# A chunked recurrence on TensorE: where the small matmuls stand between the dense ones

## The chip, the core and the metric

The kernel runs on one core of one Trainium2 chip. The metric is device microseconds of one execution, from the first to the last instruction and what lies around them; lower is better. The median of three runs of the kernel before is 1153.91 us (1153.35 to 1154.5).

## The reference, cut to what matters

Two layers over 256 tokens of width 2048. The first mixes tokens by a recurrence over 32 heads of size 64, the second is a sparse attention that the change does not touch. Of the first, what counts here:

```python
r, k, v, z = (mixed[i] @ w_rkvz[i] for i in range(4))        # four dense 2048 x 2048 products
# per head, one step per token t:
sa = S @ a_t
S = S * w_t + outer(sa, b_t) + outer(v_t, k_t)
o_t = S @ r_t
# afterwards, per head and token:
o = normalise(o) * ln_g + ln_b
bonus = sum(r * k * r_k) * v                                 # a scalar per head and token, times v
y = (o + bonus) * silu(z)
h = x + y @ w_o
```

## The kernel before, in words

**Dense products.** Every large weight is fetched as f32 by SyncE (line 178), split by ScalarE into a high part `whi` (line 206) and by VectorE into the rest `wlo` (line 191). TensorE then makes three products for each pair of operands: lines 587 to 589 (256 columns, weight as the stationary operand) or 569, 570 and 572 (512 columns). All of these use the whole 128 x 128 array.

**The recurrence.** The 256 tokens are cut into four chunks `c` of 64, the 32 heads into eight units `U` of four. Inside a chunk the recurrence is written as matrix products on blocks of 64, with the inverse of a triangular 64 x 64 matrix, which VectorE computes beforehand (`stage_t`, lines 799 to 808; its second half still runs during units 0 to 2). The four heads of a unit are packed into the quarters of the array, so that these matmuls use tiles of 64 x 64 or 128 x 64 of the array. Each is f32 and stands as two records in the trace.

A unit is a loop over twelve steps `v`; `phase(U, c, p)` is called with `c = v // 3` and `p = v % 3`:

- p = 0: for c = 0 `removal` (line 1024, 128 x 64) and then the bonus, 16 matmuls with two columns each (line 1036, 64 x 64; its operand `mb` = r times k times r_k is made by VectorE on line 963). For c > 0 eight matmuls with the state S (line 1040, 64 x 64). Then ScalarE copies the result to X (line 1042).
- p = 1: four matmuls with the inverse Yb (line 1047, 64 x 64); ScalarE copies the result to `uv` (line 1049).
- p = 2: the output's part (line 1053), the next chunk's `removal` (line 1024) and the update of the state (line 1058), all 128 x 64. VectorE makes the next S (lines 1061, 1063), ScalarE its decayed copy (line 1068). VectorE then takes statistics of the chunk's output (`stats`, line 1077).

All the results of a unit lie in one pair of PSUM banks, `PBK[U]`, one bank for each `x`: columns 0 to 63 of a bank hold what X reads, 64 to 127 what `uv` reads, 128 to 191 the state's update, from 192 on four blocks of the output O, and 448 to 455 the bonus. Two such pairs take turns. The dense product r uses two other banks, `rps[0]` and `rps[1]`, which also serve the preparation of the next unit.

Beside the unit's own steps stand three kinds of work, put at steps by tables:

- `AUX`, the preparation of unit U + 1 (`prep`): `B0` and `B1` transpose the keys (three 128 x 128 transposes each, line 993, into `rps[0]`; ScalarE copies them on line 994), `G` and `Y` finish the inverse (lines 974 and 983, 64 x 64; ScalarE copies G's result to `gs`, line 976, before Y may start), `A0` and `A1` make the products of the chunk (lines 1007 and 1009, 64 x 64, 24 matmuls each), `M0` to `M2` mask them on VectorE (line 1015). `T` turns the finished output of unit U - 1 (`turn_y`, line 1118, 64 x 64).
- `NORM`, the normalisation of unit U - 1 on VectorE and ScalarE (`finish`, lines 1085 to 1111). Its last step `z` (line 1107) is what `T` waits for.
- `fill(n)`: n times three dense matmuls of 256 columns, or their worth of 512 columns. `FILL[v]` gives n for units 0 to 5, `FILLL` for unit 6, `FILLO` for unit 7. In units 0 to 6 the dense work is the product r of later units, in unit 7 the output product.

`scale_r` (lines 962 and 963, VectorE) reads `rps[0]` in step 1 and `rps[1]` in step 6, for the next unit.

During the recurrence each engine works in the order in which the code is written (`tc.manual_schedule`), SyncE's queue included. What an instruction waits for follows from the tiles that it reads and writes. Work in the background (the second half of the inverse) is put in by a planner, `Sched`: every piece of work adds its estimated cost to a clock `sch.t`, and `sch.pump()` issues the next step of the inverse when that clock has come to its due time.

Of the kernel before, what the change touches and what calls it, by code (L numbers as in the profile page):

```python
# [13 lines left out]
OP = mybir.AluOpType  # L14
# [3 lines left out]
T, D, NK = 256, 2048, 16  # L18
LORA = 96
CH = 64  # L20
NCH = T // CH
# [47 lines left out]
W1D, CXG = 5, 1  # L69
KPO = 3  # L70
KLAG = 2
AUX = {2: ("B0",), 3: ("G",), 4: ("B1", "Y"), 7: ("A0",), 9: ("A1",), 10: ("T", "M2"), 11: ("M0", "M1")}
NORM = {1: ("nmr", "v", "02"), 2: ("b",), 5: ("24",), 6: ("46",), 7: ("68",), 8: ("g", "+"), 9: ("z",)}
FILLL = (3, 4, 4, 0, 0, 5, 0, 0, 0, 0, 0, 0)
PROLOGUE = ("R0", "R1", 6, "G", "B0", 4, "I", "Y", "B1", 2, "V6", "A0", 2, "V9", "A1", "M2", "V9", "M0", "M1", 2)
ZHOOK = 9
PACES, PACE = (0.6, 1.8, 3.0, 3.0), [0.0]
FILL = (3, 4, 4, 0, 0, 5, 4, 0, 4, 0, 4, 4)
FILLO, LASTFILL = 4, 36
QZ = (0, 25, 24, 1, 2, 23, 22, 21, 3, 20, 19, 18, 4, 17, 16, 15, 14, 13, 12, 11, 10)  # L80
SQG, XPG, W2G = 0, 1, 0
ZB = 8
# [135 lines left out]
def hybrid_kernel(ctx: ExitStack, tc: tile.TileContext, a: dict, out: bass.AP):  # L218
    nc = tc.nc
    V, S, G, PE = nc.vector, nc.scalar, nc.gpsimd, nc.tensor  # L220
    sch = Sched()
# [164 lines left out]
    W0, A0, KA, RK, KVG, BG = [prm1[:, 16 * i:16 * i + 16] for i in range(6)]  # L386
# [450 lines left out]
    R = [slice(0, 64), slice(64, 128)]  # L837
    H = lambda x, h: R[h ^ x]
    NU = NK // 2
# [16 lines left out]
    def load_y(U, eng=G, qs=(1, 0)):  # L856
        sch.require(lambda: U // 4 in tdone)
        for q in qs:
            for x in range(2):
                for h in range(2):  # L860
                    at = 64 * (h ^ x) + 32 * q
                    eng.dma_start(Yb[U % 2][at:at + 32, x, :, 32 * q:32 * q + 32],
                                inverse(yvd[U // 4], ((2 * U + x) % 8) * 2 + h, q))
# [42 lines left out]
    one = lambda name, shape: scan.tile(shape, F32, name=name)  # L906
# [4 lines left out]
    AMR = [one(f"amr{i}", [128, 2, 2, NCH, 64]) for i in range(2)]  # L911
    ARS = [[one(f"ars{i}{x}", [128, 2, NCH - 1, 64]) for x in range(2)] for i in range(2)]
    BKT = [[one(f"bkt{i}{x}", [128, NCH - 1, 2, 64]) for x in range(2)] for i in range(2)]
    mb = one("mb", [128, 2, T])
    ones2 = one("ones2", [128, 2])
    PCH, PBK, OU, GY, GS, AT, XS, STA, SST, NRM = [{} for _ in range(10)]
    mm = dict(stop=True, skip_group_check=True)
    each = [(x, h) for x in range(2) for h in range(2)]
# [8 lines left out]
    def clear_uv(U):  # L927
        for h in range(2):
            G.memset(UV[U % 2][R[h], :, :, h, :], 0.0)
# [20 lines left out]
    def parts(U, x):  # L950
        t = SPL[U % 2][x]
        return (t[:, 0:512].rearrange("p (c x t) -> p c x t", c=NCH, x=2),
                t[:, 512:512 + NCH * (CH + 1)].rearrange("p (c t) -> p c t", c=NCH),
                t[:, SPW - 512:SPW - 256],
                t[:, SPW - 256:].rearrange("p (x c t) -> p x c t", x=2, c=NCH))

    def scale_r(U, x):
        if x == 0:
            PCH[U] = scan.tile([128, 2, NCH], F32, name="pc", bufs=3)
        BK, pp, kr, ar = parts(U, x)  # L960
        pr = rps[x][:, 0:256]
        V.tensor_tensor(ar[:, 1], c3(pr), pp[:, :, 1:], op=OP.mult)
        V.tensor_tensor(mb[:, x], pr, kr, op=OP.mult)
        G.tensor_copy(PCH[U][:, x], pp[:, :, CH])
        G.tensor_tensor(ARS[U % 2][x], ar[:, :, 1:, :],
                        pp[:, None, 0:NCH - 1, CH:CH + 1].to_broadcast([128, 2, NCH - 1, CH]), op=OP.mult)
# [51 lines left out]
    def view(U, c0, n):  # L1018
        return PBK[U].rearrange("p (x c) -> p x c", x=2)[:, :, c0:c0 + n]

    def removal(U, c):
        uv, px = UV[U % 2], view(U, 0, 64)
        for x, h in each:
            PE.matmul(px[H(x, h), x], AMA[U % 2][:, x, c, :], uv[:, x, c, h, :], start=True, **mm)

    def phase(U, c, p):
        uv, px, pu, pS = UV[U % 2], view(U, 0, 64), view(U, 64, 64), view(U, 128, 64)
        O = view(U, 192 + 64 * c, 64)
        st = SST[U][0] if c else None
        if p == 0:  # L1030
            if c == 0:
                removal(U, 0)
                for i in range(NCH):
                    for x, h in each:
                        o = x * 512 + 448 + 2 * i
                        PE.matmul(PBK[U][H(x, h), o:o + 2], mb[R[h], x, 64 * i:64 * i + 64], ones2[R[h]], start=False, **mm)
            else:
                for k, o in enumerate((px, O)):
                    for x, h in each:
                        PE.matmul(o[H(x, h), x], ARS[U % 2][x][R[h], k, c - 1, :], st[R[h], x, :], start=False, **mm)  # L1040
            X = scan.tile([128, 2, 64], F32, name="X", bufs=2)
            S.activation(X, px, AF.Copy)
            XS[U] = X
            sch.t += 350
        elif p == 1:
            for x, h in each:
                PE.matmul(pu[R[h], x], Yb[U % 2][H(x, h), x, c, :], XS[U][H(x, h), x, :], start=False, **mm)
            for h in range(2):
                S.activation(uv[R[h], :, c, h, :], pu[R[h]], AF.Copy)
            sch.t += 200  # L1050
        else:
            for x, h in each:
                PE.matmul(O[H(x, h), x], AMR[U % 2][:, h, x, c, :], uv[:, x, c, h, :], start=False, **mm)  # L1053
            if c < NCH - 1:
                removal(U, c + 1)
            if c < NCH - 1:
                for x, h in each:
                    PE.matmul(pS[R[h], x], BKT[U % 2][x][:, c, h, :], uv[:, x, c, h, :], start=False, **mm)
                nxt = scan.tile([128, 2, 64], F32, name="S", bufs=3)
                if c == 0:  # L1060
                    V.tensor_copy(nxt, pS)
                else:
                    V.tensor_tensor(nxt, SST[U][1], pS, op=OP.add)
                dec = None
                if c < NCH - 2:
                    dec = scan.tile([128, 2, 64], F32, name="sP", bufs=2)
                    for x in range(2):
                        S.activation(dec[:, x], nxt[:, x], AF.Copy, scale=PCH[U][:, x, c:c + 1])
                SST[U] = (nxt, dec)
            sch.t += 700  # L1070

    def stats(U, c):
        if c == 0:
            STA[U] = (scan.tile([128, 2, 4, 6], F32, name="sta", bufs=2), scan.tile([128, 2, 4, 2], F32, name="mv", bufs=2))
        sta = STA[U][0]
        for x in range(2):
            V.bn_stats(sta[:, x, c, :], view(U, 192 + 64 * c, 64)[:, x])
# [72 lines left out]
    def fill(n):  # L1150
        budget[0] += 3 * N256 * n
        while budget[0] > 1.0:
            c = next(dense)
            budget[0] -= c
            sch.t += c
            sch.pump()
# [38 lines left out]
    for U in range(NU):  # L1195
        PBK[U] = pair_tile(U % 2)
        P = U - 1
        PACE[0] = PACES[min(U + 1, 3)]
        for v in range(12):
            phase(U, v // 3, v % 3)  # L1200
            if v % 3 == 2:
                stats(U, v // 3)
            sch.pump()
            if v == 11:
                if U + 2 < NU:
                    load_y(U + 2, qs=(1,))
                finish(U, "rg")
            if v == 0:
                if U and U + 1 < NU:
                    load_y(U + 1, qs=(0,))  # L1210
                if U + 1 < NU:
                    clear_uv(U + 1)
                    load_v(U + 1)
                if U + 2 < NU:
                    load_spl(U + 2)
            if v == 1 and U + 1 < NU:
                scale_r(U + 1, 0)
            if v == 6 and U + 1 < NU:
                scale_r(U + 1, 1)
            if U:  # L1220
                for step in NORM.get(v, ()):
                    finish(P, step)
            for step in AUX.get(v, ()):
                if step == "T":
                    if U:
                        turn_y(P)
                elif U + 1 < NU:
                    prep(step, U + 1)
            if v == 9 and U % 4 == 0:
                load_gb(U)  # L1230
            if v == 8 and U + 2 < NU:
                load_a(U + 2)
            if v == 8:
                load_rows(vt, vd, U)
            if v == 9:
                load_rows(zt, zd, U)
            fill(FILLO if U + 1 == NU else FILLL[v] if U + 2 == NU else FILL[v])
            sch.pump()
    U = NU - 1
    fill(6)  # L1240
# [216 lines left out]
    pr = accp("PT")  # L1457
# [283 lines left out]
```

## Time and profile before

| | us |
|---|---|
| median of three runs | 1153.91 |
| the profiled execution | 1155.41 |
| its span, first to last instruction | 1153.6 |
| TensorE busy | 1119.0 (97%) |
| VectorE busy | 844.8 (73%) |
| ScalarE busy | 715.8 (62%) |
| GpSimd busy | 328.3 (28%) |
| granted TensorE clock, mean | 0.992 |

The units of the recurrence begin, by line 1024 of step 0, at 371.7, 397.1, 421.7, 448.2, 473.9, 497.5, 521.5 and 542.3 us of the span; the last ends at about 570 us. In the timeline a row is: start in us, duration in us, engine, line, operation, output <- inputs, the tile of the array that is used (for matmuls), the shape, and the number of records that were merged; in brackets the idle time of the engine before it and what ended that. The matmuls of one engine are pipelined, so starts say more than durations: from one start to the next is what a matmul costs.

### The profile page before, as it was taken

Reading aid. Unit: us, or ns where it says so; the run is one execution under the profiler, and the core shown is the slowest. Engines: PE = TensorE matmul, PEld = TensorE weight load, DVE = VectorE, ACT = ScalarE, POOL = GpSimd, SP = SyncE. Lnnn points to the kernel's source line nnn. Section 1 sums busy time; section 2 is a strip of 40 time slices with the busy share of each in tenths; the row PEclk is TensorE's granted clock in tenths of the full one; section 3 lists DMA queues with packets and bytes.
Section 4 is the critical chain, followed back from the end, with each engine's and each line's share of the span. In section 5 each row is a group of like instructions: output and inputs, shape, how many; then the busy total and the mean of one; then the engine's idle time right before and its main releaser. Section 6 shows DMA issues by size and latency. Waiting matters only on the chain.

```text
span 1153.6 us, 25609 instructions
## 1 busy us (share of the span) xinstructions
PE 1119.0 (97%) x9414; PEld 979.6 (85%) x9414; DVE 844.8 (73%) x1876; ACT 715.8 (62%) x1680; POOL 328.3 (28%) x420
## 2 busy tenths in 40 slices
PE   7999999999999999998999999999999999999996
PEld 7878899888988888887788888887989989988886
DVE  6999876689897886566567876764567888775564
ACT  5767777577764466554547766665566666665553
POOL 1300045424347555653000010100333333333011
PEclk8999999999999999998999999999999999999999
DMA  6558878777879878774467667675746354645752
GB/s 232 160 186 247 236 206 262 233 216 219 259 219 277 202 218 235 217 192 121 138 213 255 199 194 260 199 243 163 198 121 163 100 135 107 165 107 176 285 186 104
DMA packets 232413, 226.31 MB, mean 196 GB/s; under 512 B 50608, under 2 KB 180000, under 8 KB 231904
## 3 DMA queue, kind: packets, MB, share of 16 engines
q1 hardware_dynamic: 227392, 219.73, 64.3%
q0 software_dynamic: 4896, 4.95, 1.9%
q8 instruction: 74, 1.21, 0.4%
q14 instruction: 51, 0.42, 0.1%
HBM read 200.48 MB, written 24.15 MB: 195 GB/s over the span
## 4 chain that ended last, share of the span: by engine, by line
PE 79%; DVE 11%; issue 3%; ACT 3%; DMA 3%; POOL 0%; SPq 0%; ACTq 0%; POOLq 0%; DVEq 0%
PE bank L570 13%; PE bank L569 13%; PE bank L572 13%; PE bank L587 7%; PE bank L589 7%; PE bank L588 7%; PE bank L234 5%; DVE wlo L191 3%; PE pair L572 1%; PE pair L569 1%; PE pair L570 1%; DVE invX L805 1%; ACT whi L206 1%; PE pair L1053 1%; DVE mtmp L426 1%
## 5 line engine op out<-in xcount | busy, mean ns | idle before, releaser
L191 DVE TENSOR_TENSOR wlo<-wraw,whi 128x512 fp32r<-128x512 f32 (+2 forms) x616 | 438.6, 725 | 149.9 <-ACT whi L206 145.2
L206 ACT ACTIVATE whi<-wraw 128x512 fp32r<-128x512 f32 (+2 forms) x664 | 402.0, 619 | 205.6 <-PE bank L572 94.5
L587 PE MATMUL bank<-mh,whi 128*128 128x256 f32 (+1 forms) x800 | 235.4, 294 | 0.8 <-ACT whi L206 0.4
L570 PE MATMUL bank<-wlo,mh 128*128 128x512 f32 (+3 forms) x608 | 229.1, 379 | 2.1 <-DVE wlo L191 2.1
L588 PE MATMUL bank<-ml,whi 128*128 128x256 f32 (+1 forms) x800 | 227.7, 285 | 0.0
L572 PE MATMUL bank<-whi,ml 128*128 128x512 f32 (+3 forms) x608 | 227.6, 377 | 0.0
L589 PE MATMUL bank<-mh,wlo 128*128 128x256 f32 (+1 forms) x800 | 227.3, 285 | 0.0
L569 PE MATMUL bank<-whi,mh 128*128 128x512 f32 (+3 forms) x608 | 202.2, 378 | 0.8 <-ACT mh L419 0.8
L587 PEld LDWEIGHTS bank<-mh,whi 128*128 128x128 f32 (+1 forms) x800 | 151.3, 189 | 7.0 <-issue 0.9
L588 PEld LDWEIGHTS bank<-ml,whi 128*128 128x128 f32 (+1 forms) x800 | 151.7, 190 | 1.8
L589 PEld LDWEIGHTS bank<-mh,wlo 128*128 128x128 f32 (+1 forms) x800 | 151.4, 189 | 1.3
L570 PEld LDWEIGHTS bank<-wlo,mh 128*128 128x128 f32 x608 | 114.3, 188 | 20.6 <-DVE wlo L191 3.3
L572 PEld LDWEIGHTS bank<-whi,ml 128*128 128x128 f32 x608 | 114.4, 188 | 17.8 <-issue 0.4
L569 PEld LDWEIGHTS bank<-whi,mh 128*128 128x128 f32 x608 | 113.4, 188 | 18.9 <-ACT mh L419 1.0
L191 POOL TENSOR_TENSOR wlo<-wraw,whi 128x512 fp32r<-128x512 f32 (+2 forms) x48 | 62.4, 1301 | 190.4 <-ACT whi L206 158.6
L570 PE MATMUL bank<-wlo,kvh 128*128 128x512 f32 x192 | 76.9, 401 | 0.0
L572 PE MATMUL bank<-whi,kvl 128*128 128x512 f32 x192 | 76.1, 396 | 0.0
L569 PE MATMUL bank<-whi,kvh 128*128 128x512 f32 x192 | 67.4, 396 | 0.0
L419 ACT ACTIVATE mh<-mtmp 128x256 fp32r<-128x256 f32 x96 | 39.0, 411 | 21.8 <-DVE mtmp L426 20.6
L426 DVE SCALAR_TENSOR_TENSOR mtmp<-xx,prm,xn 128x256 f32<-128x256 f32 x96 | 47.8, 504 | 1.2 <-POOL xx L458 1.0
L570 PEld LDWEIGHTS bank<-wlo,kvh 128*128 128x128 f32 x192 | 36.1, 188 | 8.7 <-issue 0.4
L420 DVE TENSOR_TENSOR ml<-mtmp,mh 128x256 fp32r<-128x256 f32 x96 | 41.5, 440 | 1.4 <-ACT mh L419 1.3
(332 smaller groups left out, 1871.2 us busy)
## 6 DMA issues: line engine op xcount, KB each, us to landing
wraw<-in_a_w_rkvz_dram SPq DMA_DIRECT2D x128, 512.0 KB, 5.5
wraw<-in_kv_w_dram SPq DMA_DIRECT2D x48, 512.0 KB, 4.4
wraw<-in_b_w_in_dram SPq DMA_DIRECT2D x40, 512.0 KB, 4.2
wraw<-in_a_w_o_dram SPq DMA_DIRECT2D x32, 512.0 KB, 4.6
wraw<-in_b_w_o_dram SPq DMA_DIRECT2D x32, 512.0 KB, 4.3
spd<-sp SPq DMA_DIRECT2D x16, 642.0 KB, 5.6
spl<-spd SPq DMA_DIRECT2D x16, 642.0 KB, 5.9
wraw<-in_b_w_in_dram SPq DMA_DIRECT2D x24, 384.0 KB, 3.3
```

The lines of the kernel that those rows point to most:

```text
L191: eng.tensor_tensor(lv, src, hv.bitcast(F32), op=OP.subtract)
L206: self.nc.scalar.activation(hv, src, AF.Copy)
L234: return fn(*args, **kw)
L419: S.activation(h, src, AF.Copy)
L420: V.tensor_tensor(l, src, h.bitcast(F32), op=OP.subtract)
L426: V.scalar_tensor_tensor(m, xx[:, k, :], mu[:, k:k + 1], xn[:, k, 1:], op0=OP.mult, op1=OP.add)
L569: PE.matmul(o, mh[:, ts], wh[:, 0, :], start=k == ends[0], stop=False)
L570: PE.matmul(o, mh[:, ts], wl[:, 0, :], start=False, stop=False)
L572: PE.matmul(o, ml[:, ts], wh[:, 0, :], start=False, stop=k == ends[1])
L587: PE.matmul(o, wh[:, s, :], mh, start=k == 0 and first, stop=False, **kw)
L588: PE.matmul(o, wh[:, s, :], ml, start=False, stop=False, **kw)
L589: PE.matmul(o, wl[:, s, :], mh, start=False, stop=k == NK - 1, **kw)
```

## The change

The bonus leaves step 0 and stands in step 6, behind `phase` and ahead of the planner's pump, as a function of its own that adds 430 ns to the planner's clock. Its operand `mb` gets a second buffer, since unit U + 1 now writes it while unit U has not read its own. `B1` goes from step 4 to step 5. The dense work that stood in steps 6 and 11 goes to steps 8 and 10, one fill goes from step 5 to step 0; a unit's sum is unchanged (32, 16 and 48 fills). With no dense work in step 11, the last output product of a unit (line 1053) is followed at once by the first `removal` of the next unit (line 1024).

```diff
-AUX = {2: ("B0",), 3: ("G",), 4: ("B1", "Y"), 7: ("A0",), 9: ("A1",), 10: ("T", "M2"), 11: ("M0", "M1")}
+AUX = {2: ("B0",), 3: ("G",), 4: ("Y",), 5: ("B1",), 7: ("A0",), 9: ("A1",), 10: ("T", "M2"), 11: ("M0", "M1")}
...
-FILLL = (3, 4, 4, 0, 0, 5, 0, 0, 0, 0, 0, 0)
+FILLL = (4, 4, 4, 0, 0, 4, 0, 0, 0, 0, 0, 0)
...
-FILL = (3, 4, 4, 0, 0, 5, 4, 0, 4, 0, 4, 4)
-FILLO, LASTFILL = 4, 36
+FILL = (4, 4, 4, 0, 0, 4, 0, 0, 8, 0, 8, 0)
+FILLO, LASTFILL = (4, 4, 4, 4, 4, 4, 0, 4, 8, 4, 4, 4), 36
...
-    mb = one("mb", [128, 2, T])
+    mb = [one(f"mb{i}", [128, 2, T]) for i in range(2)]
...
-        V.tensor_tensor(mb[:, x], pr, kr, op=OP.mult)
+        V.tensor_tensor(mb[U % 2][:, x], pr, kr, op=OP.mult)
...
+    def bonus(U):
+        for i in range(NCH):
+            for x, h in each:
+                o = x * 512 + 448 + 2 * i
+                PE.matmul(PBK[U][H(x, h), o:o + 2], mb[U % 2][R[h], x, 64 * i:64 * i + 64], ones2[R[h]], start=False, **mm)
+        sch.t += 430
...
                 removal(U, 0)
-                for i in range(NCH):
-                    for x, h in each:
-                        o = x * 512 + 448 + 2 * i
-                        PE.matmul(PBK[U][H(x, h), o:o + 2], mb[R[h], x, 64 * i:64 * i + 64], ones2[R[h]], start=False, **mm)
...
+            if v == 6:
+                bonus(U)
             sch.pump()
...
-            fill(FILLO if U + 1 == NU else FILLL[v] if U + 2 == NU else FILL[v])
+            fill(FILLO[v] if U + 1 == NU else FILLL[v] if U + 2 == NU else FILL[v])
```

## The prediction

> **What bounds the kernel now.** I read the page first (busy time by engine, clock, queues), then the waits of PE over the recurrence, then the timeline of PE, ACT and DVE through whole units.
>
> ```profile
> span 1153.6 us, 25609 instructions
> PE 1119.0 (97%) x9414; PEld 979.6 (85%) x9414; DVE 844.8 (73%) x1876; ACT 715.8 (62%) x1680; POOL 328.3 (28%) x420
> ...
> q8 instruction: 74, 1.21, 0.4%
> ```
>
> PE is busy for 97% of the span, so a microsecond that leaves PE's own sequence shortens the kernel, unless another engine's result is then late. The waits of PE between 372 and 570 us, the eight units of the recurrence, come to only some 10 us (who waited for whom: total us, times, longest):
>
> ```profile
> PE pair L1040 <- issue: 2.0, 1, 2.0
> ...
> PE pair L1118 <- DVE O L1107: 1.7, 4, 0.8
> PE bank L1009 <- issue: 1.7, 2, 1.1
> PE bank L993 <- DVE mb L963: 1.6, 1, 1.6
> ```
>
> So the recurrence has little idle time to win; the change must shorten PE's own work. What it aims at is the price of changing the tile size. Here are three small groups between dense matmuls, in step 8 of unit 4 (start, duration, engine and line; x counts records, of which each small f32 matmul makes two):
>
> ```profile
> 489.06 0.45 PE L1053 MATMUL pair<-uv,amr 128*64 128x64 f32 x8
> 489.34 0.40 PE L1024 MATMUL pair<-uv,ama 128*64 128x64 f32 x8
> 489.57 0.40 PE L1058 MATMUL pair<-uv,bkt 128*64 128x64 f32 x8
> 489.91 0.38 PE L587 MATMUL bank<-mh,whi 128*128 128x256 f32 x1
> 490.13 0.28 PE L588 MATMUL bank<-ml,whi 128*128 128x256 f32 x1
> 490.25 0.28 PE L589 MATMUL bank<-mh,wlo 128*128 128x256 f32 x1
> ```
>
> Read the starts. The same four matmuls take 0.23 us when the next group has their size (489.34 to 489.57) and 0.34 when dense work follows: 0.11 for the change. The first dense matmul after it takes 0.22 against 0.12 for the next: 0.10 more. So a detour out of dense work costs 0.2 to 0.3 us beside its matmuls, and the change removes such detours.
>
> **Part a, the seam between two units.** Steps 10 and 11 of unit 4 and 0 of unit 5:
>
> ```profile
> 493.85 0.39 PE L587 MATMUL bank<-mh,whi 128*128 128x256 f32 x1
> ...
> 495.48 0.45 PE L1053 MATMUL pair<-uv,amr 128*64 128x64 f32 x8
> ...
> 497.49 0.45 PE L1024 MATMUL pair<-uv,ama 128*64 128x64 f32 x8
> 497.87 0.64 PE L1036 MATMUL pair<-ones,mb 64*64 64x2 f32 x32
> 498.44 0.39 PE L587 MATMUL bank<-mh,whi 128*128 128x256 f32 x1
> ...
> 499.71 0.34 PE L1047 MATMUL pair<-X,Yb 64*64 64x64 f32 x8
> ```
>
> From 493.85 to 499.71 are 5.86 us with 12, 12 and 9 dense matmuls. After the change: 24 dense, 1.63 (493.85 to 495.48) and 12 x 0.12 more, 3.07; L1053 and L1024 side by side, 0.28 and 0.34 by the rows of step 8; 12 dense, 1.63. Sum 5.32, 0.54 less, and it holds three dense matmuls more (0.36) that step 5 gives up. Gain 0.90 at each of the six seams from units 0|1 to 5|6: -5.4. At the seam 6|7 there is no dense work beside it and PE waits for DVE's masks anyway (row 544.44 below): 0. The bonus itself isn't gone but paid in part b.
>
> **Part b, the bonus in step 6.** Unit 4, and unit 6, which has no dense work between L1040 and L1047 and so shows the bare chain:
>
> ```profile
> 485.83 0.46 PE L1040 MATMUL pair<-S,ars 64*64 64x64 f32 x16
> ...
> 487.85 0.34 PE L1047 MATMUL pair<-X,Yb 64*64 64x64 f32 x8
> ```
>
> ```profile
> 533.42 0.46 PE L1040 MATMUL pair<-S,ars 64*64 64x64 f32 x16
> ...
> 533.99 0.28 ACT L1042 ACTIVATE X<-pair 128x128 f32<-128x128 f32 x1 [0.24 <-ACT whi L206]
> ...
> 534.32 0.34 PE L1047 MATMUL pair<-X,Yb 64*64 64x64 f32 x8 [0.45 <-ACT X L1042]
> ...
> 536.57 0.29 DVE L1063 TENSOR_TENSOR S<-sP,pair 128x128 f32<-128x128 f32 x1 [2.29 <-PE pair L1058]
> 536.77 0.35 DVE L1077 BATCH_NORM_STATS2 sta<-pair 128x6 f32<-128x64 f32 x2
> ...
> 537.18 0.46 PE L1040 MATMUL pair<-S,ars 64*64 64x64 f32 x16 [0.73 <-DVE sta L1077]
> ```
>
> Now L1040 to L1047 takes 2.02, of which 12 x 0.12 = 1.44 is dense work that moves to step 8, where it only lengthens a dense run: 0.58 remains. Afterwards the bonus, 32 records, stands there: 0.57 (497.87 to 498.44) less 0.11 for the change at its end, 0.46. What decides is whether it runs while ACT makes X, or after it. X ends 0.85 after L1040's start (533.42 to 533.99 + 0.28), and L1047 can start at 0.90. The bonus writes columns 448 to 455 of the same PSUM bank of which X reads columns 0 to 63. Two places show that this kernel orders such neighbours by bank, not by column: the last L1040 above starts at 537.18, 0.06 after the statistics of other columns ended (537.12), though its own operand S was ready at 536.86; and in step 0 X waits for the whole bonus:
>
> ```profile
> 498.67 0.28 ACT L1042 ACTIVATE X<-pair 128x128 f32<-128x128 f32 x1 [0.97 <-PE pair L1036]
> ```
>
> L1024, whose columns X reads, had ended at 497.94, the bonus at 498.51. So I take it that the moved bonus waits for X: 0.85 + 0.05 + 0.46 = 1.36, and 1.40 with B1's copy, which now stands ahead of X on ACT. Cost 1.40 - 0.58 = 0.82 in units 0 to 5 (+4.9), 1.40 - 0.90 = 0.50 in unit 6, and about 0.8 in unit 7, whose dense matmuls move likewise: +6.2. The other end: a bonus that needn't wait is wholly inside the 0.90, and costs 0.32 in units 0 to 5, 0 in unit 6 and 0.3 in unit 7: +2.2. The Trainium skill speaks for the first (PSUM — Partial Sum Buffer, section "PSUM bank collisions raise a hardware error"): two engines on one bank and quadrant collide whichever columns they touch, so semaphores must guard by bank. The two rows agree with it; with waits by column the sum below would be -3.8 instead of +0.2.
>
> Who is behind the waiting bonus: PE's queue, so L1047, and A0, which must also wait until DVE has read rps[1] for mb. That read follows the last dense matmul at once and takes two operations of 0.41 (row 400.99 below), some 0.9 us, before A0 starts at 1.56: hidden.
>
> **Part c, B1 leaves the place between L1047 and Y.**
>
> ```profile
> 481.64 0.34 PE L1047 MATMUL pair<-X,Yb 64*64 64x64 f32 x8
> 481.92 0.55 PE L993 MATMUL bank<-cst,spl 128*128 128x128 f32 x3
> 482.39 0.67 PE L983 MATMUL pair<-gs,t 64*64 64x32 f32 x32
> ```
>
> ```profile
> 481.80 0.38 ACT L976 ACTIVATE gs<-pair 128x256 f32<-128x256 f32 x1 [0.20 <-PE pair L974]
> ```
>
> The transposes were not only a change of size, they covered ACT's copy gs, which Y needs. From L1047 to Y are 0.75 now. Without them Y waits until 482.18 + 0.05 = 482.23, 0.59: 0.16 won. B1 beside dense work in step 5 costs 0.47 - 0.11 = 0.36 at most. So +0.2 where gs is that late, and a gain of up to 0.2 where ACT has it early, as L1047 itself waited longer for X. Seven units, bounds -1.4 to +1.4; taken +0.4, nearer to the row.
>
> **Part d, waits on DVE.**
>
> ```profile
> L191 DVE TENSOR_TENSOR wlo<-wraw,whi 128x512 fp32r<-128x512 f32 (+2 forms) x616 | 438.6, 725 | 149.9 <-ACT whi L206 145.2
> ```
>
> Twelve dense matmuls more in step 8 give DVE 1.44 us, less one wlo more (0.7), before turn_y (L1118) needs O. Its waits in the row above are 1.7 in four places; unit 6, without dense work, keeps its own:
>
> ```profile
> 539.23 0.69 PE L1118 MATMUL pair<-cst,O 64*64 64x64 f32 x32 [0.53 <-DVE O L1107]
> ```
>
> The rest goes: -1.2. Given back: step 11 loses its dense work, so DVE's chain from the statistics over the masks to mb has less cover before B0 in step 2.
>
> ```profile
> 395.10 0.45 PE L1053 MATMUL pair<-uv,amr 128*64 128x64 f32 x8
> ...
> 402.07 0.55 PE L993 MATMUL bank<-cst,spl 128*128 128x128 f32 x3
> ```
>
> ```profile
> 400.99 0.41 DVE L963 TENSOR_TENSOR mb<-bank,spl 128x256 f32<-128x256 f32 x1
> ```
>
> At the seam 0|1 mb is ready at 401.40, 0.67 before B0. PE's way there, 6.97, shrinks to 0.28 + 0.34 + 1.63 + 0.28 + 1.63 + 0.85 = 5.01, 1.96 less. DVE sheds one wlo and about one step of the inverse, 1.2 (estimate): 0.1 short, and 1.3 if it sheds nothing. This counts in units 1 and 2, while the inverse runs; taken +0.6 in all. In unit 0 B0 already waits 1.6 for mb, so the bonus that leaves its step 0 wins nothing but room for three dense matmuls: -0.4. The second buffer of mb lifts a wait that no row shows: 0. No DMA is added; loads that step 6's and 11's dense work asked for are asked for in 8 and 10, behind the load of vt that waits for DVE. Five buffers stand ahead; 0.
>
> ```profile
> 544.44 0.79 PE L569 MATMUL pair<-whi,mh 128*128 128x512 f32 x1 [0.25 <-DVE amr L1015]
> ```
>
> **Sum:** -5.4 + 6.2 + 0.4 - 1.2 + 0.6 - 0.4 = +0.2 us. The profiled execution took 1155.41 (span 1153.6 and 1.8 around it), the median of the runs is 1153.91; the sum goes on the median: 1154.1. A measurement of this kernel can tell about 0.2%, 2.3 us, from no change.
>
> **Rivals.** *The bonus runs inside X's wait* (if order is by column): -5.4 + 2.2 + 0.4 - 1.2 + 0.6 - 0.4 = -3.8, 1150.1. Against it stand the two rows on banks. Of changes of tile size alone it is the count: 21 a unit before, 14 after. The Trainium skill says that each drains the array (TensorEngine Tiling (Array Packing), section "Tiling Modes"), and the 0.11 and 0.10 above agree; by that rule alone the change is this gain or more.
>
> *PE's instructions arrive too late* (slower). The stalls "issue" of 2.0 and 1.7 lie between equal matmuls that wait for no engine. The page's instruction queue moved 1.21 MB in 74 packets, 16 KB each, for 2 x 9414 instructions: one packet feeds 254, or 127 matmuls. The new stretch L1040, bonus, L1047, A0 and the three groups of step 8 is 16 + 32 + 8 + 48 + 24 = 128 records, a whole packet, in 1.40 + 0.16 + 1.04 + 0.85 = 3.4 us (the 0.16 and 1.04 are from 487.85 on to 489.06, 1.21 in all). It decides once a packet needs over 3.4 us; a stall of 1.2, the mean of the three seen, in each of units 0 to 5, less the 3.7 that are there now, gives +3.5: 1157.6. For it: the stalls exist, all in such stretches. Against: steps 9 and 10 get longer dense runs on both sides, which thins out their stretch. The Trainium skill holds that crossing a 16 KB block is mostly hidden (Runtime: NRT & Kernel Launch, section "Instruction fetch mechanics"); the 2.0 us row is one that is not.
>
> *The stalls fall elsewhere and vanish*: -3.7 + 0.2, 1150.4; what speaks for it is only that three in eight units is chance. *DVE is late at B0 in every unit up to 3*, by the 1.3 of the upper bound at four seams, less the 0.6 already counted: 0.2 + 5.2 - 0.6 = +4.8, 1158.7. Against it, DVE's load falls after the inverse (units 1 and 4; after the length stand PE, PEld and DVE busy):
>
> ```profile
> 396.00:421.00 25.00, 24.22 (x500) 22.04 (x500) 20.66 (x50) 13.98 (x40) 14.87 (x23) 1.00 0.77 201
> ```
>
> ```profile
> 473.00:497.00 24.00, 23.80 (x499) 21.70 (x499) 15.67 (x43) 14.02 (x41) 14.89 (x24) 1.00 0.65 171
> ```
>
> **How the numbers follow.** Forecast, no change that can be told, 1154.1 (its own range 1151.7 to 1156.3): 0.52. Bonus hidden 0.13 and stalls gone 0.12: faster 0.25. Instructions late 0.17 and DVE late 0.06: slower 0.23. The range runs from 1150.2 to 1157.7, about from the faster cases to the late instructions.
>
> **What would show it.** After the change: in unit 4 L1040 to L1047 of step 6 should be 1.3 to 1.5 us, with L1036 starting 0.9 after L1040 behind ACT's X; if L1036 follows at 0.3, part b is wrong and the gain is some 4 us. L1053 and L1024 at the seam should be 0.28 apart. Y should start some 0.05 after gs ends, with an idle PE before it. L1118 should wait for DVE in unit 6 alone. PE's "issue" waits over the recurrence should stay near 3.7 after unit 0's start; two more or fewer decide the sign.

## The result, and the profile after

The changed kernel takes 1159.68 us (median of 8 runs, 1157.24 to 1162.87) against 1153.83 for the kernel before (8 runs, 1149.18 to 1154.5): a ratio of 1.0053, 95% interval 1.0037 to 1.0069. It is slower, by some 5.9 us; the forecast was 1154.1, its range ended at 1157.7. The profiled execution took 1157.91 (span 1156.1). In the changed kernel the lines of the phases stand three later: 1043, 1045 and 1050 for 1040, 1042 and 1047, then 1056, 1061, 1064, 1080, 1102, 1110 and 1121 for 1053, 1058, 1061, 1077, 1099, 1107 and 1118; the bonus stands on 1030.

From the page of the changed kernel, the span, the engines and the instruction queue:

```profile
span 1156.1 us, 25619 instructions
...
PE 1114.4 (96%) x9414; PEld 977.8 (85%) x9414; DVE 839.6 (73%) x1876; ACT 714.7 (62%) x1680; POOL 329.6 (29%) x420
...
q8 instruction: 74, 1.21, 0.4%
```

PE is busy for 4.6 us less than before, and yet the span is longer: PE waits more. The waits of PE over the recurrence in the changed kernel (who for whom: total us, times, longest):

```profile
PE pair L1043 <- DVE sta L1080: 4.9, 4, 3.5
PE pair L1030 <- ACT X L1045: 4.2, 8, 0.6
PE bank L993 <- DVE mb L963: 2.8, 2, 2.0
...
PE pair L569 <- DVE amr L1015: 1.6, 1, 1.6
PE pair L1121 <- DVE O L1110: 1.0, 2, 0.5
```

Four of the five were in the forecast: the bonus behind X, B0 behind `mb`, the dense work of unit 7 behind `amr`, T behind O. The first was not. One wait of 3.5 us stands in step 3 of unit 3. PE and VectorE there:

```profile
453.34 0.28 PE L589 MATMUL bank<-mh,wlo 128*128 128x256 f32 x1
457.09 0.46 PE L1043 MATMUL pair<-S,ars 64*64 64x64 f32 x16 [3.47 <-DVE sta L1080]
```

```profile
450.82 0.16 DVE L1100 SCALAR_TENSOR_TENSOR nmr<-mv,rg 128x8 f32<-128x8 f32 x1
455.18 0.69 DVE L1102 TENSOR_TENSOR vt<-vt,bon 128x512 f32<-128x512 f32 x1 [4.21 <-DMA vt<-vd]
455.79 0.68 DVE L191 TENSOR_TENSOR wlo<-wraw,whi 128x512 fp32r<-128x512 f32 x1
456.39 0.28 DVE L1064 COPY S<-pair 128x128 f32<-128x128 f32 x1
456.60 0.35 DVE L1080 BATCH_NORM_STATS2 sta<-pair 128x6 f32<-128x64 f32 x2
```

Read them upwards from PE. L1043 waited for VectorE's S and statistics; these stood in VectorE's queue behind the product `vt` times `bon` of the unit before; and that waited 4.21 us for a load of `vt` that had not landed. So the question goes to SyncE, which issues it. Its queue in the changed kernel, and then in the kernel before:

```profile
434.40 0.38 SPq L178 DMA_DIRECT2D wraw<-in_a_w_rkvz_dram  x1
445.03 1.39 SPq L1287 DMA_DIRECT2D xl<-in_x_dram  x3
446.52 0.42 SPq L946 DMA_DIRECT2D vt<-vd  x1
446.98 1.30 SPq L948 DMA_DIRECT2D vt<-vd  x2
448.38 0.54 SPq L178 DMA_DIRECT2D wraw<-in_a_w_rkvz_dram  x1
```

```profile
442.69 0.34 SPq L946 DMA_DIRECT2D vt<-vd  x1
443.08 1.69 SPq L948 DMA_DIRECT2D vt<-vd  x2
...
445.50 0.52 SPq L946 DMA_DIRECT2D zt<-zd  x1
446.08 1.09 SPq L948 DMA_DIRECT2D zt<-zd  x2
447.34 1.49 SPq L1282 DMA_DIRECT2D xl<-in_x_dram  x3
```

Three loads of 512 KB have changed places. They fetch x for the residual at the end of the first layer (`residual`, line 1287; 1282 before), long ahead of need, into memory that the inverse's tiles give back. Their code stands behind the part that is kept in the written order, so the scheduler puts them into SyncE's queue by its own estimate of the time, and in the changed kernel they came to stand ahead of unit 2's `vt`. That the changed estimates did this is inferred: the diff touches nothing else that could. There they wait for the inverse's last result to be stored (issued at 440.81), and SyncE, which issues in order, stood from 434.78 to 445.03. So `vt` was issued 5.8 us after VectorE had last read its buffer (440.7); before, at once (442.66). After that it travelled beside 1.5 MB of x, and landed 7.5 to 8.0 us after its issue; before, 2.3 to 5.2. Nothing else in SyncE's order differs. Which of the three parts of the change (the bonus, B1, the dense work) moves the estimates that far is not shown: the runs below that take them apart pin these loads.

What came behind the wait is the second surprise. Windows of the changed kernel with the granted clock (after the five busy times):

```profile
453.00:457.00 4.00, 0.62 (x6) 0.41 (x4) 1.82 (x6) 0.29 (x2) 1.62 (x4) 1.00 1.17 229
457.00:465.00 8.00, 7.70 (x143) 7.22 (x143) 2.71 (x7) 5.11 (x16) 0.00 (x0) 0.57 1.08 294
```

PE stood for 3.4 of 4 us, and from 458.09 to 464.92 it ran at half clock. From L1043 of step 3 to L1043 of step 6 went 7.47 us (457.09 to 464.56), in unit 4 4.83: 2.6 us more, on top of the wait. (With the loads of x back in their place, a run below, unit 3 itself takes 5.16 there, so 2.3 more.) The kernel before had one such stretch inside the recurrence, 541.39 to 548.22, behind its waits in units 6 and 7; the changed kernel has a shorter one there, 546.83 to 550.25.

The parts that the forecast did price came out much as it said. The seam between units 4 and 5:

```profile
500.35 0.45 PE L1056 MATMUL pair<-uv,amr 128*64 128x64 f32 x8
500.63 0.40 PE L1024 MATMUL pair<-uv,ama 128*64 128x64 f32 x8
500.96 0.39 PE L587 MATMUL bank<-mh,whi 128*128 128x256 f32 x1
...
502.59 0.34 PE L1050 MATMUL pair<-X,Yb 64*64 64x64 f32 x8
```

0.28 and 0.33 for the two groups side by side; with the first dense matmul at 497.28 the whole is 5.31, where 5.32 was expected. Step 6 of unit 4:

```profile
487.89 0.46 PE L1043 MATMUL pair<-S,ars 64*64 64x64 f32 x16
...
488.58 0.28 ACT L1045 ACTIVATE X<-pair 128x128 f32<-128x128 f32 x1
...
488.91 0.64 PE L1030 MATMUL pair<-ones,mb 64*64 64x2 f32 x32 [0.56 <-ACT X L1045]
489.37 0.21 PEld L1050 LDWEIGHTS pair<-X,Yb 64*64 64x64 f32 x8
489.40 0.32 PE L1050 MATMUL pair<-X,Yb 64*64 64x64 f32 x8
```

The bonus waits for X, 1.02 after L1043, and L1050 follows at 1.51 instead of 1.40.

### The profile page after: what moved, and what is told of

It is laid out like the page before. It is cut to its first block, busy times and chain, and to the rows that moved or that the text cites. A ratio compares the mean times of both kernels' runs of the same rounds, so it can differ in the third digit from the quotient of the medians.

```text
span 1156.1 us, 25619 instructions
## 1 busy us (share of the span) xinstructions
PE 1114.4 (96%) x9414; PEld 977.8 (85%) x9414; DVE 839.6 (73%) x1876; ACT 714.7 (62%) x1680; POOL 329.6 (29%) x420
## 4 chain that ended last, share of the span: by engine, by line
PE 77%; DVE 10%; ACT 4%; issue 3%; DMA 3%; POOL 1%; SPq 0%; ACTq 0%; POOLq 0%; DVEq 0%
PE bank L569 13%; PE bank L570 13%; PE bank L572 13%; PE bank L587 7%; PE bank L588 6%; PE bank L589 6%; PE bank L234 5%; DVE wlo L191 3%; PE pair L572 1%; PE pair L569 1%; PE pair L570 1%; ACT whi L206 1%; DMA wraw<-in_a_w_rkvz_dram 1%; PE pair L1056 1%; DVE mtmp L426 1%
```

## The experiments

Two theories. **One:** the loads of x in the new place, their wait and the half clock behind it make the change slow. **Two:** the change's own steps do, the bonus in front of X above all. All ratios are to the kernel before, run beside it on the same chip.

**The place of the loads of x, in both kernels.** In the changed kernel this edit holds the loads back; in the kernel before a dependency the other way round holds unit 2's `vt` until they are issued:

```diff
-    xls = [residual(nb, ops[nb]) for nb in range(3)]
+    with tc.issue_after(xl_after[0]):        # the last load of unit 2's zt
+        xls = [residual(nb, ops[nb]) for nb in range(3)]
```

> The changed kernel, but the three loads of x for the residual (xl) are queued on SyncE behind unit 2's load of zt, where they stood before, instead of ahead of its load of vt. Theory 1 (the place of these loads): the wait of L1043 in unit 3 (3.5 us) and the half clock that follows (6.8 us long) go, and the time comes back to within 0.2% of the kernel before, 1152 to 1156 us. Theory 2 (the change's own steps: the bonus behind X, less cover for DVE): it stays 4 us or more slower than before.

> The kernel before, but the loads of xl are queued ahead of unit 2's load of vt, as they stand in the changed kernel; nothing else moves. Theory 1: 4 to 7 us slower than before, with a wait of 3 us or more of PE for DVE in step 3 of unit 3 and a stretch of half clock behind it. Theory 2: no change, within 1 us.

Measured: the changed kernel with the loads back, 1154.57, ratio 1.0020 (1.0010 to 1.0030); the kernel before with the loads early, 1157.75, ratio 1.0051 (1.0038 to 1.0063). So the place of three loads alone makes the kernel before as slow as the change, and taking it back wins about three fifths of the change's loss. The trace of the first shows the chain undone, SyncE and VectorE:

```profile
442.87 0.34 SPq L946 DMA_DIRECT2D vt<-vd  x1
...
447.68 1.55 SPq L1290 DMA_DIRECT2D xl<-in_x_dram  x3
```

```profile
453.06 0.68 DVE L1102 TENSOR_TENSOR vt<-vt,bon 128x512 f32<-128x512 f32 x1
```

`vt` is there when VectorE comes to it. In the kernel before with early loads L1040 of unit 3 waits 3.76 us for the same reason. Theory one holds for the larger part; 0.2% is left, where 0.2 us was forecast.

**The loads of x in unit 5**, behind its `zt` (the same edit, with U == 5), in both kernels:

> The changed kernel with the loads of xl behind unit 5's load of zt. Theory 1: like the loads behind unit 2's zt or 1 to 2 us better, as the transfers of units 2 and 3 are then alone: 1151 to 1155 us. Theory 2: 4 us or more slower than before.

> The kernel before with the loads of xl behind unit 5's load of zt. Theory 1: within 0.2% of before, or up to 2 us better where the transfers of units 2 and 3 had cost something. It also tells by how much the changed kernel differs when neither has these loads in units 2 and 3: the sum of the prediction gives +0.2 us for that difference, theory 2 gives 4 us or more.

Measured: 1157.37, ratio 1.0040 (1.0028 to 1.0053), and 1153.87, ratio 1.0012 (1.0004 to 1.0021). The first is a miss for theory one: no load is late in its trace by more than 0.5 us, and it is slower than with the loads in unit 2. What its trace shows is half clock four times inside the recurrence, at 376.92, 411.05, 530.52 and 544.17, behind waits that other runs have too, but for a stall of 1.57 us ahead of the third. That asked for a third theory. **Three:** the granted clock halves for a window of 3.41 us when PE stood for too much of the window before, and the change adds waits that carry windows over that limit.

The runs list the mean granted clock of each execution, so its part can be taken off: (1 - clock) times the span, averaged over a kernel's runs, is what half clock can have cost. It is an upper bound, since half clock costs nothing where PE waits anyway. Against the kernel before beside it, in us of the mean:

| kernel | longer by | of it clock | rest |
|---|---|---|---|
| change, loads of x back | 2.3 | 1.9 | 0.4 |
| change, loads of x in unit 5 | 4.3 | 4.0 | 0.3 |
| before, loads of x early | 5.5 | 3.1 | 2.4 |
| before, loads of x in unit 5 | 1.2 | 1.3 | -0.1 |

By the scatter of the runs, each rest here and below is known to 1 to 1.7 us. The rest is 0.3 to 0.4 for the change whose loads are out of the way, and 2.4 for the early loads. In the change itself (mean clock 0.9894, 12.3 us) the clock's part is 3.7 to 4.0 by the 8.3 to 8.6 that the kernel before shows on four chips.

**The parts one by one**, the loads of x pinned behind unit 2's `zt` in all four:

```diff
 # seam_alone: the kernel before with
+FILL = (4, 4, 4, 0, 0, 4, 4, 0, 4, 0, 8, 0)
 # bonus6_alone: the kernel before with bonus(U) at v == 6, two mb, FILLO of the change, and
+FILL = (3, 4, 4, 0, 0, 5, 0, 0, 8, 0, 4, 4)
 # change_b1_back: the change with 4: ("B1", "Y") again
 # seam_bonus7: FILL as in seam_alone, B1 back, unit 7 as before, and behind A0 in step 7
+                    if step == "A0":
+                        bonus(U)
```

> The kernel before with step 11's dense work moved to step 10 (and one of step 5's units to step 0); the bonus stays in step 0, B1 in step 4, and the loads of x are pinned where they stand before. By my terms the seam gains 0.90 less the 0.46 of the bonus that stays, 0.44 at six seams, 2.6, and B0's waits for mb give back 0.6: 2.0 us faster, ratio 0.998. By the rival (the stretches between dense runs get longer, and mb comes late) the gain is eaten: B0 waits over 1 us in units 1 and 2 and there are more issue stalls; ratio 1.000 to 1.001.

> The kernel before with the bonus alone moved to step 6 (mb in two buffers, step 6's dense work in step 8, the last unit as in the change), loads of x pinned where they stand before. By my terms step 6 costs 0.82 more in units 0 to 5 and 0.5 in unit 6, step 0 saves the bonus's 0.46 seven times, unit 7 costs 0.8 less the 0.46, T waits 1.0 less: 4.9 + 0.5 - 3.2 + 0.3 - 1.0 = 1.5 us slower, ratio 1.0013. If the bonus in front of the wait for X is what makes the change slow beyond my terms (short waits next to late instructions, then half clock), it is 3 us or more slower, ratio 1.0026 or more.

> The changed kernel with B1 back in step 4 and the loads of x pinned where they stand before; beside it stands the changed kernel with the x loads pinned, at ratio 1.0020. By my terms B1's move cost 0.4 us, so ratio 1.0017. If B1's copy on ACT ahead of X in step 6 is what costs (X ended 0.97 after L1043 instead of 0.85), another 0.7 comes back, ratio 1.001. If B1's move is not what is left, no difference from 1.0020.

> The changed kernel's seam, but the bonus stands behind A0 in step 7, where X has been read and A0 covers the copies of uv, B1 back in step 4, step 6's dense work back, the last unit as before, loads of x pinned as before. By my terms: six seams -5.4, seven bonuses at 0.46 = +3.2, B0's waits +0.6, unit 0 -0.4: 2.0 us faster than before, ratio 0.998. If what is left of the slowdown is the seam itself and not the bonus's wait for X, the ratio stays at 1.001 to 1.002.

| kernel | ratio (95%) | longer by | of it clock | rest |
|---|---|---|---|---|
| seam alone | 0.9993 (0.9978 to 1.0009) | -1.0 | 0.5 | -1.5 |
| bonus in step 6 alone | 1.0056 (1.0035 to 1.0077) | 6.3 | 4.4 | 1.9 |
| change, B1 back | 1.0032 (1.0017 to 1.0048) | 3.5 | 2.9 | 0.6 |
| seam, bonus behind A0 | 1.0009 (0.9994 to 1.0023) | 1.4 | 0.8 | 0.6 |

By the rest, the seam is worth 1.5 where 2.0 was expected and the bonus costs 1.9 where 1.5 was: within that scatter the terms stand. By the time that counts, the seam alone can't be told from the kernel before, and the bonus alone costs as much as the whole change, without any load of x in the way; that is the second outcome of its expectation, 3 us or more, and theory two has a part in it. The trace of the bonus alone shows one more accident, on VectorE and ScalarE:

```profile
440.10 0.68 DVE L808 TENSOR_REDUCE invT<-invX 128x32 f32<-128x512 f32 x1
...
440.81 2.29 ACT L830 ACTIVATE invA<-invT 128x256 f32<-128x256 f32 x4 [3.07 <-DVE invT L808]
443.00 1.13 ACT L206 ACTIVATE whi<-wraw 128x512 fp32r<-128x512 f32 x2
444.04 0.26 ACT L1045 ACTIVATE X<-pair 128x128 f32<-128x128 f32 x1
```

The four copies that end the inverse stand ahead of X in step 9 of unit 2 in the kernel before as well, but there VectorE's last step of the inverse is done by 434.7 and ScalarE goes through them without a wait. Here that step came to stand behind what step 8 gives VectorE, and ScalarE waited 3.07 us for it; PE waited 1.78 us for X, and ran at half clock from 445.53 for 3.41 us. B1's return brought nothing that can be told: its ratio lies above the 1.0020 of the change with the loads back, the intervals overlap, and its trace has an accident of its own, a wait of 1.50 us of line 974 for the load of Yb in unit 3 and half clock from 456.63 for 6.83 us. In the last one the bonus waits for nobody, but PE stands at places where it waits for no engine, as the rival with the late instructions had it; PE's waits from 360 to 573 there, and then in the seam alone:

```profile
PE pair L1007 <- issue: 2.9, 1, 2.9
...
PE bank L1009 <- issue: 1.7, 1, 1.7
```

```profile
PE pair L1007 <- issue: 1.8, 1, 1.8
...
PE bank L1009 <- issue: 1.0, 1, 1.0
```

Both stand in step 9, in units 3 and 5, and at these places the kernel before has 1.15 and 0.52. So the stalls are not new, but longer; one profiled execution of each kernel can't show that the bonus makes them so.

**Filling the waits.** If theory three is right, matmuls whose result nobody reads, put into waits that exist anyway, must make the kernel faster. The waits at the end of the recurrence stand in every kernel here (the edit, shortened):

```diff
+    def warm(n):                              # rps[0] is free there, keep is a ready y
+        for _ in range(n):
+            PE.matmul(rps[0][:, 0:256], keep[:, 0:128], keep[:, 0:256], start=True, **mm)
...
+            warm({(NU - 2, 9): 6, (NU - 1, 0): 16}.get((U, v), 0))
             phase(U, v // 3, v % 3)
...
+                        if U == NU - 2:
+                            warm(4)
                         turn_y(P)
```

> The kernel before with 26 matmuls more, whose result nobody reads, in PE's waits at the end of the recurrence: 6 ahead of L1040 in step 9 of unit 6, 4 ahead of T, 16 ahead of L1024 of unit 7. Clock theory: a 3.41 us window in which PE stood for over 1.6 us is followed by one at half clock; the waits 538 to 542 are filled, so the stretch at half clock from 541.39 on (6.83 us) goes, and about half of it is won: 2.5 to 3.4 us, ratio 0.997 to 0.998. Rival, only the waits themselves cost: nothing is won (the matmuls stand in waits), ratio 1.000 to 1.001.

> The changed kernel with the loads of x back behind unit 2's zt (1.0020 without more), and the same 26 matmuls, and 10 more behind L1024 of unit 7, where the dense work waits 1.6 for amr. Clock theory: the windows 538 to 549 stay at full clock, ratio 0.998 to 0.999. Rival, only the waits cost: 1.002 to 1.003.

> The seam alone (0.9993 without more) with the same 26 matmuls. Clock theory: ratio 0.996 to 0.997, the fastest of all. Rival: 0.999 to 1.000.

Measured: 0.9981 (0.9969 to 0.9992), 0.9998 (0.9985 to 1.0011) and 0.9970 (0.9951 to 0.9989; 1149.7 us). All three are 0.2% faster than without the matmuls, as theory three has it, by a little less than it expected in the first two; the rival expected nothing. The first gain is measured against the kernel before on the same chip; for the other two, the runs without the matmuls were on other chips and the intervals touch or overlap. The mean clock agrees: its part against the kernel before is -2.4, -1.9 and -2.0 us with the matmuls; without them it was 1.9 and 0.5 in the second and third. The windows 538 to 546 and 546 to 554 of the kernel before, and then of the same with the matmuls:

```profile
538.00:546.00 8.00, 5.23 (x118) 4.42 (x113) 6.16 (x18) 2.73 (x9) 1.67 (x1) 0.71 0.24 68
546.00:554.00 8.00, 8.00 (x71) 5.60 (x70) 3.61 (x9) 3.67 (x10) 0.00 (x0) 0.86 0.22 69
```

```profile
538.00:546.00 8.00, 6.97 (x114) 5.67 (x109) 6.17 (x18) 2.70 (x8) 1.67 (x1) 1.00 0.23 68
546.00:554.00 8.00, 8.00 (x81) 5.71 (x80) 3.44 (x8) 4.85 (x13) 0.00 (x0) 1.00 0.41 138
```

VectorE and ScalarE do the same work in both; PE, busy with nothing of use, keeps its clock at 1.00, and in the second window 81 matmuls pass instead of 71. (This execution met half clock elsewhere, from 461.52 for 3.41 us, behind a wait of 2.08 us for a `whi` in unit 3.) The seam alone with filled waits is faster than both kernels.

**The wait of unit 3, filled.** A first try put 48 such matmuls ahead of L1043 in step 3 of unit 3 of the changed kernel, into `rps[0]`:

> The changed kernel as it is, loads of x in front, with 48 matmuls of 128 columns (2.6 us by the rate of the dense ones) ahead of L1043 in step 3 of unit 3, inside the wait of 3.47 us that the late vt makes there. Clock theory: the wait stays, the half clock from 458.09 on (6.83 us, some 2.5 us lost) goes: 2.5 us faster than the changed kernel, ratio to before 1.003. Rival, the wait alone costs: no difference from the change, 1.005.

Measured: 1171.11, ratio 1.0162 (1.0142 to 1.0182). It says nothing on its question:

```profile
458.02 10.50 PE L1036 MATMUL bank<-mh 128*128 128x128 f32 x48 [4.24 <-ACT bkt L994]
```

The bank was not free: the added matmuls waited for ScalarE's copy of B0, which stood behind the decayed copy of the same late S. They began when the wait was over, 10.5 us on the path: 0.22 us each where 0.054 was expected, and half clock accounts for a factor of two of that; the rest stays open. The second try took the pair of banks that A has left, 24 matmuls of 256 columns, in the changed kernel and in the kernel before with early loads:

```diff
+            if (U, v) == (3, 3):
+                idle = pair_tile(2)
+                for _ in range(24):
+                    PE.matmul(idle[:, 0:256], keep[:, 0:128], keep[:, 0:256], start=True, **mm)
```

> The changed kernel as it is, loads of x in front, with 24 matmuls of 256 columns (0.12 each, 2.9 us) that nobody reads ahead of L1043 in step 3 of unit 3, in the pair of PSUM banks that A has left, which waits for nothing. Clock theory: the wait for the late vt stays, but PE works in it, so the half clock from 458.09 on (6.83 us, some 2.5 us lost) goes: ratio to before 1.003 instead of 1.005. Rival, the wait alone costs: 1.005.

> The kernel before with the loads of x ahead of unit 2's vt (1.0051 without more) and the same 24 matmuls ahead of L1040 in step 3 of unit 3. Clock theory: the half clock from 454.09 on (6.83 us) goes, the wait of 3.8 us stays: ratio 1.003. Rival: 1.005.

Measured: 1.0037 (1.0022 to 1.0052) and 1.0022 (1.0006 to 1.0037), where the same without them had 1.0053 and 1.0051. In the trace of the first:

```profile
457.21 3.04 PE L1207 MATMUL pair<-mh 128*128 128x256 f32 x24
460.67 0.46 PE L1043 MATMUL pair<-S,ars 64*64 64x64 f32 x16 [0.42 <-DVE sta L1080]
```

The wait is still there, filled, and no half clock follows. In the second, 1.5 us of the wait stayed open in the profiled execution, and half clock still followed, at 458.13. The gains are 1.8 and 3.3 us against 2.5 expected; they were measured on another chip than the runs without the matmuls, and for the changed kernel the two intervals overlap. Over all runs the clock's part fell from 3.7 to 4.0 us to 1.8 in the changed kernel, and from 3.1 to 1.3 in the other. So some 2 to 3 us of the loss at this place is the clock, as much as the 2.4 of the wait; the size is known no better than that.

## Why the prediction was wrong, point by point

- **Part a, the seam: right.** 5.31 us measured in unit 4 for 5.32 worked out. Alone, with the bonus left in place, it gave 1.5 us at full clock (known to about 1 us); in the time that counts nothing that can be told.
- **Part b, the bonus: right in its mechanism, a little small.** Order is by bank, as the two rows and the Trainium skill (PSUM — Partial Sum Buffer, section "PSUM bank collisions raise a hardware error") said: the bonus starts 1.02 after L1043, behind X. 1.51 instead of 1.40, since ScalarE now does a `whi` beside B1's copy ahead of X: 0.1 us a unit. Unit 7 cost what was forecast: steps 6 and 8 together, from L1043 to L1050 and from L1061 to the next L1043, take 4.72 for 3.90, 0.82 where 0.8 stood. Its wait for `amr` rose from 0.25 to 1.61, but only because the bonus no longer fills it: from L1024 to the first dense matmul go 2.15 us in both kernels. It is idle time of PE all the same, and counts for the clock.
- **Part c, Y: the mechanism right, the size not told apart.** In unit 4 Y starts 0.05 after `gs` ends, 0.57 after L1050 (0.59 worked out). B1's return changed nothing measurable.
- **Part d, waits on VectorE: sizes off by under a microsecond.** T's waits fell from 1.7 to 1.0, not to 0.5. B0 waited 1.97 in unit 0 and 0.80 in unit 2, together 2.8 instead of 1.6, where +0.6 was taken.
- **The step that failed** is the last one of part d, "No DMA is added; loads that step 6's and 11's dense work asked for are asked for in 8 and 10, behind the load of vt that waits for DVE. Five buffers stand ahead; 0." It looked at the loads that the moved work asks for, and not at those that belong to nobody there. SyncE's queue changed in the place of three loads of x, outside the diff, and this put a load that VectorE needs in unit 3 behind them: 2.4 us without the clock's part.
- **The term that was missing** is the clock. The sum counted a wait by its length. The mean granted clock is 0.9894 in the changed kernel and 0.9925 to 0.9928, by chip, in the kernel before: 3.7 to 4.0 us at most. 1.9 of it is still there when the loads of x are back; the longer waits of B0, of `amr` and of the bonus stand in that kernel, and that they cause it is argued, not shown. With 2.4 for the wait and 0.4 for the change's own steps this makes 6.5 to 6.8, against 5.9 by the medians and 6.8 by the means; terms that are each known to a microsecond or more can't do better.
- **The change's own sum** of +0.2 was +0.4 at full clock with the loads of x back, and +1.3 in the pair with filled waits (1.5 against 0.2 longer, by the same subtraction).
- **The rivals.** The bonus inside X's wait: excluded by the 1.02. Instructions late: not in this change, whose stalls of more than half a microsecond after unit 0's start are 0.74 and 0.56 in the profiled execution, where the forecast had 3.7. The longest of all, 2.9, stands in the kernel with the bonus behind A0. The stalls did fall away, and the time rose all the same: the sentence that two stalls "decide the sign" was wrong. VectorE late: it was late in unit 3, by more than was feared, and not for its load but for a DMA.

Open stays why the change with the loads of x in unit 5 met half clock more often than with them in unit 2 (five runs), and which part of the change's own 1.9 us of clock belongs to which wait.

## What to carry to other kernels

Where a scheduler places work by estimated times, a change of costs anywhere can move loads that the diff doesn't touch: compare the order of every queue before the sum is made, and pin what is long and not urgent behind what is small and due. Price a wait of TensorE with the clock that it may cost behind it, and fill waits that can't be removed. A change that wins PE a few tenths of a microsecond per unit, as the seam here, is best tried alone, without the parts that add waits: alone it could not be told from no gain, and with filled waits its kernel was the fastest of all by the median (1149.7 us).

## What the runs showed of the hardware

**The granted clock goes by windows.** In the 16 profiles the clock changes at multiples of 3.41 us only. Lay that grid over PE's idle time, from the half clock at the start of each execution to PE's last matmul: of the windows at full clock in which PE stood for 1.7 us or more all 25 were followed by one at half clock, between 1.2 and 1.7 us it was 7 of 28, below 1.2 us none of some 5,100. So in these kernels it took some 1.2 to 1.7 us of idle time in a window, a third to a half of it, in one wait or in several (1.62 us out of two waits in the kernel before, in the window from 537.98). The grid has another phase in each execution, so the same wait of 2.0 us (B0 in unit 0) is followed by half clock in one execution and, split between two windows, not in another; this can make part of the spread between runs. The Trainium skill (TensorE: Matmul & The Clock Gate, section "HAM oscillation — how this bites in real kernels") puts the limit at idle gaps of over some 3.4 us; here the windows with 1.7 to 2 us decide.

**A large load in front slows small ones.** Behind three loads of 512 KB, unit 2's loads of `vt`, of 64 and 128 KB, took 7.5 to 8.0 us to land in the changed kernel and 7.8 to 8.0 in the kernel before with early loads; ahead of them they took 2.3 to 5.2 in the kernel before and 2.8 to 5.1 in the change with the loads back.
